# Early loads and an interleaved first projection in an eight-core hybrid decoder step

## The chip, the cores and the metric

The kernel runs on the 8 NeuronCores of one Trainium2 chip. Each core takes one prompt of 2048 positions and 16 single-token samples, 2064 columns in all; no core talks to another. The metric is the device time of the slowest core in microseconds (us). Engines are named as in the profile: PE is TensorE, PEld its weight loads, DVE is VectorE, ACT is ScalarE, POOL is GpSimd, SP the SyncE queue.

Some executions fall in a slow state, in which the cores of one die get a lower clock: 1585.82 us with 0.819 to 0.835 on one die is an example.

## The reference, cut to what matters

Two layers, of which only the first part of the first is touched by the change: RMSNorm, one input projection, a pooling mixer and a short convolution, then the output projection.

```python
def run_group(x, ...):                       # layer 0
    h = rmsnorm(x, norm_mix[0])
    z = h @ w_in_even[0]                     # 1024 -> 512 pool | 512 conv x | 512 B gate | 512 C gate
    p, xb, bg, cg = jnp.split(z, [...], axis=-1)
    a_out, ph = pool_mixer(pool_hist, p, start, w_pool, pool_scale)   # windows 2, 4, 8, 16
    b_out, ch = conv_mixer(conv_hist, xb, bg, cg, conv_w)             # bg * conv3(cg * xb)
    mix = jnp.concatenate([a_out, b_out], axis=-1) @ w_out_even[0]
    x = x + mix
    ...                                      # FFN, layer 1, FFN, final norm: not touched
```

## The kernel before: the parts that matter

x lies feature-major in SBUF, in 8 slabs of 128 features (index `k` or `c`), cut along the columns into five tiles `n` of 256, 512, 512, 512 and 272. A small scheduler gives every instruction the semaphore waits that follow from the buffers that it reads and writes; each engine runs its instructions in the order of the program text. So the order of the text is the order on each engine, and that is what the change moves.

The loads (before):

```python
for q in range(2):                      # x tile 0, two halves, on the SP queue
    x0ev.append(sc.dma("sp", xT[...tile 0, half q], ..., sem=f"xin0_{q}"))
for q in range(2):                      # pooling weights: wait for half 0 of x tile 0
    sc.dma("pool", wring[0][:, q*2048:(q+1)*2048], ..., writes=[wpB[q]], extra=[x0ev[0]])
for q in range(4):                      # x tile 1 in quarters: the first waits for weights half 0
    sc.dma("sp", xT[...tile 1, quarter q], ..., extra=([wpB[0].w] if q == 0 else []))
for n in range(2, 5):                   # x tiles 2 to 4
    sc.dma("sp", xT[:, xrange_(n)], ...)
```

The first projection (before): for all five tiles the pooling products, then four conv chunks `j`, each over five tiles.

```python
spin(18); n_sq(0); n_ones(0); n_apply(0)   # spin: dummy matmuls; n_sq: squares; n_ones: their sum on PE
for n in range(5):                          # n_apply: Ln, Exp on ACT, then 8 products on DVE
    n_sq(n + 1)
    ...                                     # 32 pooling matmuls, n_ones(n + 1) among them (tile 0: after)
    n_apply(n + 1)
    ...                                     # ACT empties the 4 PSUM banks; pooling tasks are set aside
for j in range(4):                          # conv chunks
    if j == 3: use_banks(6)                 # banks 6 and 7 kept for the fold
    for n in range(5):
        ...                                 # x, C, B products: 3 banks, 24 matmuls
        ...                                 # ACT: copy of x; DVE: C * x; ACT: first tap
        for t_ in slots_of.get((j, n), []): tasks.pop(t_)()     # pooling tasks on DVE
        if back: conv_back(*back.pop())     # DVE: two taps, product with B (frees the B bank)
        if j == 3 and n != 2: fold(...)     # 2 matmuls into banks 6 and 7, ACT copies them out
```

Three terms: the dummies (`spin`) are matmuls of ones with zeros that only keep PE at work; a pooling task is DVE's running sum of one channel group over one tile; the fold multiplies `w_pool` and its scale into the output projection's weights, in eight small matmuls.

A matmul result goes to the next of 8 PSUM banks by a counter (`nbank`). A bank can be written again when its last reader is done; this is where PE waits for ACT and DVE.

## Time and profile before

| | before |
|---|---|
| time, median of 4 runs | 1340.77 us (1339.65 to 1341.65) |
| profiled run, slowest and fastest core | 1338.6 and 1334.0 us |
| PE busy in the slowest core | 1298.0 us, 97% |

The prediction below shows the lines and reads them. Two words on how: in a windows table each row is a stretch of time, with the busy time of each engine; in a timeline each row is a group of instructions with its start, its length, and in brackets how long the engine stood idle before it and what released it. For PE a low clock hides in the busy time: 16 matmuls of 512 columns take 3.61 us or, at half clock, nearly twice that, and both count as busy.

### The profile page before, as it was taken

The page shows a single profiled execution, that of the slowest core. Times are in us where ns is not written, and L with a number is a line of the kernel's source. Part 1 is how long each engine was busy: PE and PEld are TensorE (multiplying, and loading weights), DVE is VectorE, ACT ScalarE, POOL GpSimd, SP SyncE. Part 2 cuts the span into 40 slices and gives each one's busy share as a digit, 9 for nine tenths or more (in the row PEclk, how much of TensorE's full clock was granted, in tenths as well). Part 3 has the DMA queues.
Part 4 walks back from the last instruction along what each step waited for, and adds up shares of the span by engine and source line. Part 5 has one row for each costly group of instructions (what it writes and reads, how often), then busy time and mean ns, then how long its engine had stood idle before and what let it go on. Part 6 is the DMA issues. An engine that isn't in the chain of part 4 may idle for free.

```text
span 1338.6 us, 21583 instructions; the slowest of 8 cores (1334.0 to 1338.6 us)
## 1 busy us (share of the span) xinstructions
PE 1298.0 (97%) x7316; PEld 721.1 (54%) x7420; DVE 666.5 (50%) x1167; ACT 346.7 (26%) x668; POOL 169.6 (13%) x220
## 2 busy tenths in 40 slices
PE   6999999999999999999999999999999999999994
PEld 3555545555555555556454665555655556555552
DVE  3588767223527235532764775721262532745266
ACT  2532343111010110012576334411101011010154
POOL 2400153000000000000521005300000000000044
PEclk8999999999999999999999999999999999999998
DMA  8533203122111223102160101221132111220105
GB/s 217 147 62 59 54 1 64 32 44 52 32 32 33 44 53 63 32 16 42 23 127 1 35 5 28 43 53 32 32 58 39 33 32 32 56 40 16 33 33 223
DMA packets 11323, 68.67 MB, mean 51 GB/s; under 512 B 2080, under 2 KB 2208, under 8 KB 5184
## 3 DMA queue, kind: packets, MB, share of 16 engines
q0 software_dynamic: 6912, 47.19, 19.3%
q1 hardware_dynamic: 3728, 19.47, 4.2%
q8 instruction: 63, 1.03, 0.3%
q10 hardware_dynamic: 576, 0.62, 0.1%
q14 instruction: 44, 0.36, 0.1%
HBM read 105.84 MB, written 9.18 MB: 86 GB/s over the span
## 4 chain that ended last, share of the span: by engine, by line
PE 92%; DVE 3%; DMA 2%; issue 2%; ACT 1%; SPq 0%; DVEq 0%; POOL 0%; ACTq 0%; POOLq 0%
PE bank L748 63%; PE bank L818 17%; PE bank L842 5%; PE bank L1173 4%; PE bank L986 2%; DMA xTs<-xT 1%; DVE xTs L671 1%; DMA wring<-wts 1%; PE bank L1229 1%; PE bank L642 0%; DVE xTs L756 0%; PE bank L900 0%; DVE sqall L1070 0%; DVE sqall L1067 0%; DVE gtmp L936 0%
## 5 line engine op out<-in xcount | busy, mean ns | idle before, releaser
L748 PE MATMUL bank<-hTs,wring 128*128 128x512 bf16 (+2 forms) x4105 | 728.8, 337 | 4.0 <-DVE mix L1077 0.9
L748 PEld LDWEIGHTS bank<-hTs,wring 128*128 128x128 bf16 x4160 | 405.4, 98 | 318.5 <-issue 2.8
L799 DVE TENSOR_TENSOR mix<-bank,gtmp 128x512 bf16<-128x512 f32 (+2 forms) x220 | 129.4, 588 | 465.2 <-PE bank L748 459.6
L756 DVE TENSOR_TENSOR xTs<-bank,xTs 128x512 f32<-128x512 f32 (+2 forms) x480 | 278.6, 587 | 89.8 <-PE bank L748 33.8
L796 ACT ACTIVATE gtmp<-bank 128x512 f32<-128x512 f32 (+2 forms) x220 | 112.9, 514 | 712.7 <-PE bank L748 694.6
L818 PE MATMUL bank<-mix,wring 128*128 128x512 bf16 (+2 forms) x1264 | 223.8, 337 | 0.8
L818 PEld LDWEIGHTS bank<-mix,wring 128*128 128x128 bf16 x1280 | 125.3, 98 | 98.0
L125 POOL DMA_DIRECT2D wring<-wts x46 | 25.0, 543 | 941.5 <-PE bank L748 411.6
L631 POOL TENSOR_TENSOR sqall<-sqall 128x512 f32<-128x512 f32 (+5 forms) x110 | 106.5, 968 | 131.6 <-ACT sqall L627 125.2
L748 PE MATMUL bank<-mix,wring 128*128 128x512 bf16 (+2 forms) x632 | 112.9, 337 | 1.7 <-DVE mix L1077 1.2
L748 PEld LDWEIGHTS bank<-mix,wring 128*128 128x128 bf16 x640 | 62.4, 98 | 50.9 <-issue 1.8
L842 PE MATMUL bank<-mix,wring 128*128 128x512 bf16 (+2 forms) x472 | 85.0, 337 | 0.4
L627 ACT ACTIVATE sqall<-xTs 128x512 bf16<-128x512 f32 (+2 forms) x110 | 59.7, 546 | 69.6 <-DVE xTs L756 64.0
L671 DVE SCALAR_TENSOR_TENSOR hTs<-xTs,vecs_s,bank 128x512 bf16<-128x512 f32 (+2 forms) x120 | 73.7, 637 | 1.8 <-ACT bank L652 1.8
L842 PEld LDWEIGHTS bank<-mix,wring 128*128 128x128 bf16 x480 | 47.0, 98 | 36.6
L986 PE MATMUL bank<-hTs,wring 128*128 128x512 bf16 (+2 forms) x158 | 33.0, 369 | 8.1 <-DMA wring<-wts 4.8
L1173 PE MATMUL bank<-mix,hTs 128*128 128x512 bf16 (+1 forms) x135 | 31.9, 379 | 0.1
L1173 PE MATMUL bank<-wring,hTs 128*128 128x512 bf16 (+1 forms) x131 | 31.5, 379 | 0.3
L1217 ACT ACTIVATE gtmp<-bank 128x512 f32<-128x512 f32 (+2 forms) x40 | 20.6, 514 | 42.7 <-PE bank L748 26.6
L748 PE MATMUL bank<-hTs,mix 128*128 128x512 bf16 (+2 forms) x156 | 30.5, 337 | 0.2
L915 DVE SCALAR_TENSOR_TENSOR hTs<-xTs,vecs_s,bank 128x512 bf16<-128x512 f32 (+2 forms) x40 | 22.7, 640 | 15.4 <-ACT bank L911 15.4
L986 PEld LDWEIGHTS bank<-hTs,wring 128*128 128x128 bf16 x160 | 16.6, 106 | 23.6 <-issue 13.0
(95 smaller groups left out, 495.7 us busy)
## 6 DMA issues: line engine op xcount, KB each, us to landing
wring<-wts POOLq DMA_DIRECT2D x38, 1024.0 KB, 8.8
yT<-xTs SPq DMA_DIRECT2D x3, 2048.0 KB, 6.6
xTs<-xT SPq DMA_DIRECT2D x2, 2048.0 KB, 17.9
xTs<-xT SPq DMA_DIRECT2D x6, 512.0 KB, 7.0
wring<-wts POOLq DMA_DIRECT2D x4, 768.0 KB, 7.9
wring<-wts POOLq DMA_DIRECT2D x4, 512.0 KB, 6.4
mix<-wts POOLq DMA_DIRECT2D x2, 1024.0 KB, 18.9
xTs<-xT SPq DMA_DIRECT2D x1, 1088.0 KB, 23.6
```

Source lines behind the costliest of these rows:

```text
L125: E.dma_start(out=out, in_=in_, **kw).then_inc(s, 16)
L627: sc.op("act", lambda E: E.activation(out=rng[i][:, 0:w], in_=xs(c, n), func=AF.Square), reads=[xB[c][n]], writes=[rngB[i]])
L631: sc.op("pool", lambda E: E.tensor_tensor(out=dst[:, 0:w], in0=acc[a][:, 0:w], in1=rng[i][:, 0:w], op=ALU.add), reads=[accB[a], rngB[i]], ...
L671: sc.op("dve", lambda E: E.scalar_tensor_tensor(out=out, in0=xs(c, n), scalar=vecs[:, self.gcol + c:self.gcol + c + 1], in1=r_[:, 0:w], op ...
L748: last = E.matmul(bk[:, 0:w], lhsT=wt[:, o:o + 128], rhs=src_[:, k, c0:c0 + w], start=(k == 0), stop=(k == nk - 1))
L756: sc.op("dve", lambda E: E.tensor_tensor(out=xs(m, n), in0=bk[:, 0:w], in1=xs(m, n), op=ALU.add), reads=[bkB, xB[m][n]], writes=[xB[m][n]])
L796: sc.op("act", lambda E, bg_=bg_, gi=gi, w=w: E.activation(out=gtmp[gi][:, 0:w], in_=bg_[:, 0:w], func=AF.Silu), reads=[bgB], writes=[gtmp ...
L799: sc.op("dve", lambda E, bu_=bu_, gi=gi, w=w, c0=c0, slot=slot: E.tensor_tensor(out=mix[:, slot, c0:c0 + w], in0=bu_[:, 0:w], in1=gtmp[gi] ...
L818: last = E.matmul(bk[:, 0:w], lhsT=wt[:, jl * 1024 + m * 128: jl * 1024 + (m + 1) * 128], rhs=mix[:, slot, c0:c0 + w], start=(jl == 0), st ...
L842: last = E.matmul(bk[:, 0:w], lhsT=wt_[:, jl * 1024 + m * 128: jl * 1024 + (m + 1) * 128], rhs=mix[:, s0 + jl, c0:c0 + w], start=(i == 0), ...
L986: last = E.matmul(bks[g][0][:, 0:w], lhsT=wt[:, k * 512 + g * 128:k * 512 + (g + 1) * 128], rhs=hT[:, k, c0:c0 + w], start=(k == 0), stop= ...
L1173: last = E.matmul(bk[0:ntok, :], lhsT=hT[:, k, t0:t0 + ntok], rhs=wv[:, k * 512:(k + 1) * 512], start=(k == 0), stop=(k == KC - 1))
```

## The change

Its intent is to have PE in steady work earlier and never short of it. The loads of x tile 1, of the pooling weights and of the first conv weights are issued at once on the POOL queue, without waits, in the order in which they are needed. Conv chunk 0 is moved in between the pooling products, so that PE has other work while x tiles 2 to 4 arrive. More dummies bridge the time to tile 1. The last conv chunk keeps all 8 banks, and the fold uses banks that its neighbour tile has freed.

```diff
-        for q in range(2):
-            x0ev.append(sc.dma("sp", xT[:, xrange_(0, 4 * q, 4 * q + 4)], ...))
+        sc.dma("sp", xT[:, xrange_(0)], d_x[:, xrange_(0)], ..., sem="xin0")
...
+        xload(1, 2, "xin1")                     # on the POOL queue, no waits
+        for q in range(4):
+            sc.dma("pool", wring[0][:, q * 1024:(q + 1) * 1024], ...)
+        w_issue()                               # weights of conv chunk 0
+        def late_loads():
+            xload(2, 2, "xin2"); cload("hp", hp, d_hp, eng="pool")
+            xload(3, 1, "xin3"); xload(4, 1, "xin4"); w_issue()
...
+        spin(18); n_sq(0); n_ones(0); n_apply(0, VC_NMIX)
+        spin(34)
+        n_sq(1); late_loads(); ...; n_ones(1); n_apply(1, VC_NMIX)
+        for k in range(4): pool_k(0, k)
+        for n, k in ((0, 4), (0, 5), (1, 0), (1, 1), (0, 6), (1, 2), ...): pool_k(n, k)
+        pool_drain(0); pool_drain(1)
+        n_sq(2, range(4)); conv_front(0, 0); ...; n_sq(2, range(4, 8)); conv_back(...)
+        conv_front(0, 1, late=lambda: n_ones(2)); n_apply(2); early_setup(); rest(); conv_back(...)
+        before = {2: [(1, 0), (2, 0)], 3: [(3, 0), (1, 1)], 4: []}
+        for n in range(2, 5):
+            n_sq(n + 1); pool_banks(n)
+            for k in range(KC): pool_k(n, k)
+            pool_drain(n)
+            for t_ in before[n]: bg.pop(t_)()   # pooling tasks, ahead of n_apply(n + 1) on DVE
+            conv_front(0, n, hook=lambda: n_ones(n + 1))
+            n_apply(n + 1)
+            rest(); conv_back(*bkn)
...
-            if j == 3:
-                use_banks(6)
-                bk, bkB = banks[6 + g % 2], bankB[6 + g % 2]        # in fold
+                bk, bkB = bks[g % 2]                                # the x and C banks of the tile before
```

(Condensed: whole statements are joined on a line, arguments are left out, and the moved buffers of scratch data and the new split of tile 2's squares, part of them now on DVE, are not shown.)

## The prediction

> **What bounds the kernel now.** I read the page first, then the table of windows over the first 150 us, then the waits of the TensorE, then the timeline of the start. The page of before (slowest core):
>
> ```profile
> span 1338.6 us, 21583 instructions; the slowest of 8 cores (1334.0 to 1338.6 us)
> PE 1298.0 (97%) x7316; PEld 721.1 (54%) x7420; DVE 666.5 (50%) x1167; ACT 346.7 (26%) x668; POOL 169.6 (13%) x220
> ...
> PE   6999999999999999999999999999999999999994
> ...
> PEclk8999999999999999999999999999999999999998
> ```
>
> PE is 97% busy; only the first and the last of the 40 slices are below 9. The change touches nothing after the first output projection (about 155 us), so all it can win lies in the first slices. The windows of that stretch (columns: us, then busy us and count of PE, PEld, DVE, ACT, POOL, the granted clock, DMA share, GB/s written):
>
> ```profile
> 0.00:10.00 10.00, 7.68 (x26) 3.12 (x26) 1.52 (x4) 2.93 (x6) 2.81 (x15) 1.00 0.45 114
> 10.00:14.80 4.80, 0.01 (x1) 0.04 (x2) 3.22 (x8) 0.82 (x2) 0.00 (x0) 0.99 1.01 162
> 14.80:24.00 9.20, 9.15 (x50) 5.70 (x51) 0.69 (x1) 1.26 (x2) 1.04 (x1) 0.82 0.97 236
> 24.00:30.50 6.50, 1.85 (x6) 0.49 (x6) 2.37 (x4) 2.96 (x7) 2.11 (x2) 0.84 1.01 328
> 30.50:41.00 10.50, 10.43 (x37) 4.26 (x39) 5.67 (x9) 3.46 (x7) 4.68 (x6) 0.78 0.99 336
> 41.00:63.00 22.00, 21.32 (x115) 11.03 (x115) 13.73 (x27) 11.80 (x25) 10.04 (x12) 1.00 0.50 103
> 63.00:87.00 24.00, 23.84 (x145) 14.09 (x146) 16.72 (x38) 9.61 (x29) 1.97 (x5) 1.00 0.35 65
> 87.00:150.00 63.00, 59.29 (x319) 31.17 (x323) 49.72 (x79) 19.13 (x37) 1.07 (x2) 1.00 0.23 45
> ```
>
> PE's busy time here flatters: 6.80 and 3.40 us of it are the dummy warming matmuls, and at clock 0.78 to 0.84 it does useful work at down to half speed. DMA is half idle in the first 10 us, then saturated to 41 us. The timeline shows why:
>
> ```profile
> 6.98 1.25 POOL L125 DMA_DIRECT2D wring<-wts  x2 [4.84 <-DMA xTs<-xT]
> ...
> 14.79 5.27 PE L986 MATMUL bank<-hTs,wring 128*128 128x256 bf16 x32 [4.83 <-DMA wring<-wts]
> ...
> 26.61 0.63 ACT L885 ACTIVATE sqall<-xTs 128x512 bf16<-128x512 f32 x1 [3.38 <-DMA xTs<-xT]
> ...
> 30.52 5.92 PE L986 MATMUL bank<-hTs,wring 128*128 128x512 bf16 x16 [2.54 <-DVE hTs L915]
> ```
>
> Loads are chained: half of x tile 0, then the pool weights (issued only at 6.98), then x tile 1 (issued when the first weight half lands, 14.6), whose last quarter lands at 26.6 because tiles 2 to 4 queued beside it. PE does 32 matmuls at half clock (14.8 to 20), dummies, scraps, and starts tile 1 at 30.5 cold: 16 matmuls take 5.92 us, where later 16 take 3.61. From 30.5 PE is the bound, less its waits:
>
> ```profile
> PE bank L1048 <- DVE mix L1077: 3.0, 1, 3.0
> PE bank L748 <- DVE mix L1077: 2.1, 3, 1.2
> ```
>
> These (60 to 175 us) are the projection's tail: a fold matmul waits 3.0 us at 129 to 132 for a PSUM bank that a lagging VectorE has not emptied.
>
> **What the Trainium skill says.** *TensorE: Matmul & The Clock Gate*, "What's actually happening": the array runs at half clock until a busy window of about 3.4 us has passed, and falls back after an idle one. The trace agrees in kind: 0.50 at 16 to 18 us after an empty 10.0 to 14.8, 0.50 again at 30.5 after 1.85 busy us in 6.5. *DMA: Bandwidth & Descriptors*, "Queues, rings and completion order": each engine serves the queues in turn and one queue's ring in order. So tile 1 shared with tiles 2 to 4 only by ring order and with weights by turns; arrivals at 20.2, 22.6, 24.2, 26.6 fit. Same page, "Specifications": about 358 GB/s of HBM per core; the saturated windows give 328 and 336. *PSUM — Partial Sum Buffer*, "The four PSUM rules": a start flag clears the accumulation bits of the whole bank, so two 256-wide groups may share a bank if only the first starts it, which is what the changed code does; no run shows more of it yet.
>
> **The change part by part.** (a) Loads. One 1 MB load of x tile 0; at once, on the Pool queue without waits, x tile 1 (2 MB), pool weights (2 MB read, 1 MB written) in quarters, the first conv weights (1.5 MB read); then tiles 2 to 4 behind them. (b) Dummies: 18 as before, then 34 in place of 16. (c) Order: pool products of tiles 0 and 1, then conv chunk 0 of tiles 0 and 1, then for tiles 2 to 4 pool and conv 0 by turns. So PE has conv work while later tiles arrive. (d) One scratch buffer fewer (the conv x is copied straight into the conv buffer and multiplied in place); same count of instructions. (e) Conv chunks keep all 8 banks; the fold uses the two banks that the previous tile freed early. No arithmetic on PE is taken away.
>
> Arrivals, as estimates. x tile 0: before, its bytes flowed from about 2.7 us and it was wholly seen at 8.15. Weights issued at 6.98 began to move at about 9.7, 2.7 later; so tile 1, issued at about 2.1, moves from 4.8. Until then tile 0 has moved 0.5 MB; the other 0.54 MB at half of 330 GB/s takes 3.3 us: done at 8.1, seen at 8.9. Tile 1: 3.15 MB in all, the 2.64 left at 4.8 take 8.0 us: seen near 13.7. Pool weights: 2.1 MB at about 323 read GB/s (162 written in 10 to 14.8, twice that read) 6.5 us: 20; conv 0 weights: 25; tile 2: 31.5.
>
> PE: squares of tile 0 on two engines, 4 x 0.38 = 1.5 us, and its sum of ones ends at 10.7. 34 dummies x 0.216 (3.61/16 less overhead) = 7.3: 18.0. In this time VectorE applies the norm of tile 0 (11.8 to 15.0, 8 x 0.4) and squares its three of tile 1 (3 x 0.69: 17.1), so the ones of tile 1 are free to run: 8 x 0.216 = 1.7: 19.7. Pool tile 0: 32 x 0.109 = 3.5: 23.2. Pool tile 1: 32 x 0.216 = 6.9: 30.1; its inputs come at 0.67 us per k against 0.86 of use. Ones of tile 2: 1.7: 31.9. Before has the same set (pool 0 and 1, ones 0 to 2) done at 41.0. Gain 9.1 us.
>
> From 41.0 to 63.06 before does pool 2 to 4 and ones 3, 4: 6.9 + 6.9 + 3.7 + 1.7 + 0.95 = 20.2 of 22.0 us; the rest are waits for ACT to empty banks. In the new order a cycle takes 4 + 3 + 1 = 8 banks, so pool banks were emptied long ago: gain 1.8.
>
> The fold's 3.0 us wait goes (its banks are emptied by a copy and by the first VectorE product of the tile before), and part of the other 2.1; the first output products still wait for the last conv products, since the last pooling task now stands ahead of them. Gain 3.4.
>
> New stalls: tile 2's normed input comes 0.3 to 0.5 us late after conv 0 of tile 1 (ones in the middle of it, then Ln and Exp 1.3, one apply 0.7, against 1.7 us of PE work left); small bank waits. I allow 1.2. Sum: 9.1 + 1.8 + 3.4 - 1.2 = 13.1 us, 1340.8 - 13.1 = 1327.7; I say 1328.
>
> **The rivals.** *Tile 0 late and PE cold.* If turn-taking brings tile 0 at 11 instead of 8.9, PE is empty from 9.1 to 12.5 and goes cold: 34 dummies then take 7.3 + 2.5 and end near 22.5. The fixed count makes this a loss of 4 us: 1332. For it: tile 0 moved at 240 GB/s before, less than the later rate, and all eight cores start together. Against: tile 1 cannot start before 4.5. *VectorE becomes the bound.* By its rows a conv tile costs it 0.69 + 0.75 + 0.75 + 0.69 = 2.9, a pooling task 1.27 + 0.69; per cycle with a 5.4 apply it has 11.3 of PE's 13.8, and in chunks 1 to 3 about 19.5 of 20.9. That is near; if latencies add, waits of 3 to 5 us return: 1332. Against: before, chunk 0 had the most tasks (20.8) and lost only 0.4. *Transfers bind still.* Tile 2 must be seen by about 34 for its ones at 36.5; my estimate leaves 2.5. At 280 GB/s instead of 330 it comes at 36.5, and PE waits 2 to 3 us, 1330; a Pool queue that can't hold seven loads would be worse. *Better than said:* every wait but 1 us goes and the start holds: 1325.
>
> **Range and chances.** 2% would be 26.8 us. All that PE loses in before is the first 30.5 us less 6.2 of useful work at full clock (ones 0 and 1: 1.0 + 1.7, pool 0: 3.5), 2.3 of cold clock after, and waits of 1.8 and 5.1: 33.5 us; of these at least the 10.7 until tile 0's sums stay, so 2% is out of reach. The rivals cost 2 to 5 us each and more than one may come, so the range is skewed up: 1323 to 1334. Faster by over 2% 0.01, within 2% 0.98, slower 0.01.
>
> **What would show it.** Start: first pool matmul near 19.7 at clock 1.00 (wrong if over 22 or at 0.5); tile 0's first square near 8.9; pool 0 and 1 done near 30. Middle: no wait of pool matmuls for ACT; chunk 1 starts near 74 (before: 84). Tail: no 3 us wait at the fold. After it, the same stages a constant 13 us earlier. I would be wrong if PE waited on x tile 2, if clock under 0.8 stayed past 20 us, or if conv waits on VectorE summed to over 3 us.

## The result, and the profile after

The changed kernel takes 1330.52 us in the median of 10 runs (two of them slow), against 1340.95 of before in the same rounds (15 runs, three of them slow); the fast runs alone have medians of 1330.51 and 1340.79. The ratio of the fast runs is 0.9924, with a 95% interval of 0.9914 to 0.9934: 10.2 us, 0.8% faster. A ratio here is the mean time of one kernel's fast runs over that of the other's in the same rounds, so it is not quite the ratio of the medians. A later measurement of both on one chip gave 1330.32 against 1341.12, 0.9921.

The page of the changed kernel, to be set beside the first fence of the prediction:

```profile
span 1329.0 us, 21718 instructions; the slowest of 8 cores (1327.2 to 1329.0 us)
...
PE   8999999999999999999999999999999999999994
...
PEclk9999999999999999999999999999999999999997
```

The spread of the cores has shrunk too: 1.8 us instead of 4.6. The windows of the same stretches as in the prediction:

```profile
0.00:10.00 10.00, 6.62 (x18) 2.38 (x19) 0.55 (x2) 2.05 (x4) 5.31 (x21) 1.00 0.74 193
10.00:14.80 4.80, 4.80 (x25) 2.43 (x26) 3.19 (x9) 2.74 (x7) 1.04 (x1) 1.00 0.97 280
14.80:24.00 9.20, 9.20 (x56) 5.32 (x55) 4.81 (x10) 1.87 (x3) 5.64 (x7) 1.00 1.08 171
...
30.50:41.00 10.50, 9.81 (x58) 5.41 (x57) 4.36 (x9) 5.86 (x12) 3.08 (x3) 1.00 0.99 337
41.00:63.00 22.00, 20.36 (x94) 9.14 (x95) 19.20 (x33) 7.70 (x16) 8.48 (x9) 1.00 0.34 78
...
```

The clock column is the first thing to see: it is 1.00 in every row, where before it was 0.82, 0.84 and 0.78 from 14.8 to 41 us. The DMA share is 0.74 in the first 10 us instead of 0.45. But from 41 to 63 us PE is busy for 20.36 us of 22, less than before (21.32), while DVE is at 19.20 instead of 13.73: the bottleneck has moved closer to DVE there. The timeline of the start:

```profile
9.44 1.34 ACT L893 ACTIVATE sqall<-xTs 128x256 bf16<-128x256 f32 x4 [5.90 <-DMA xTs<-xT]
...
11.15 7.50 PE L973 MATMUL bank<-mix,ones 128*128 128x512 bf16 x34
...
20.22 10.56 PE L994 MATMUL bank<-hTs,wring 128*128 128x256 bf16 x64
...
56.62 5.56 PE L994 MATMUL bank<-hTs,wring 128*128 128x512 bf16 x25 [1.63 <-DVE hTs L922]
```

L893 is the squaring of x tile 0, L973 the dummies, L994 the pooling products. All 64 pooling matmuls of tiles 0 and 1 run in one piece of 10.56 us from 20.2 us on; before, the first half of them took 5.27 us, part of it at half clock, and the second began at 30.5. The last line is the flaw: pooling tile 3 waits 1.6 us for its first normed slice. The waits of PE up to 175 us in all:

```profile
PE bank L994 <- DVE hTs L922: 2.3, 2, 1.6
...
PE bank L758 <- DVE mix L1068: 1.2, 2, 0.8
PE bank L758 <- DVE mix L961: 0.9, 1, 0.9
PE bank L758 <- ACT wring L1040: 0.9, 1, 0.9
```

The fold's 3.0 us wait of before is gone; a wait for the fold's copies (ACT, L1040), one for the norm (L922) and one for a conv bank (L961, inferred) are new in their places.

To put this in stages, three points are read off the PE timelines of the slowest cores (core 2 before, core 0 after). The third is the start of the run of output-projection matmuls after their last wait for DVE.

| stage ends with | before | after | gain in the stage |
|---|---|---|---|
| pooling of tiles 0 and 1 and the sums of tiles 0 to 2 | 41.0 | 32.5 | 8.5 |
| conv chunk 0 | 83.8 | 77.2 | -1.9 |
| output projection unblocked | 156.24 | 146.53 | 3.1 |
| end | 1338.6 | 1329.0 | -0.1 |

(32.5 is 30.8, where the pooling of tiles 0 and 1 ends, plus 1.7 for the sums of tile 2, which the new order does later. 83.8 is 62.9 plus 120 matmuls at the durations in the prediction, 20.9 us. 77.2 is 76.28 plus eight 272-column matmuls.) From the third point to the end every core of both kernels needs 1181.8 to 1182.8 us, as predicted: the rest is not touched.

### The profile page after: what moved, and what is told of

The parts are those of the page before. It is cut to its first block, busy times and chain, and to the rows that moved or that the text cites. A ratio compares the mean times of both kernels' runs of the same rounds, so it can differ in the third digit from the quotient of the medians.

```text
span 1329.0 us, 21718 instructions; the slowest of 8 cores (1327.2 to 1329.0 us)
## 1 busy us (share of the span) xinstructions
PE 1302.3 (98%) x7438; PEld 721.9 (54%) x7438; DVE 671.4 (51%) x1170; ACT 344.9 (26%) x667; POOL 174.6 (13%) x227
## 4 chain that ended last, share of the span: by engine, by line
PE 92%; DVE 5%; issue 1%; ACT 1%; DMA 1%; DVEq 0%; POOL 0%; ACTq 0%; POOLq 0%
PE bank L758 63%; PE bank L828 17%; PE bank L852 5%; PE bank L1230 4%; DVE hTs L922 1%; DVE xTs L681 1%; PE bank L994 1%; DMA xTs<-xT 1%; PE bank L973 1%; PE bank L1286 1%; PE bank L652 0%; DVE xTs L766 0%; PE bank L907 0%; DVE gtmp L943 0%; DVE sqall L1061 0%
## 5 line engine op out<-in xcount | busy, mean ns | idle before, releaser
L758 PEld LDWEIGHTS bank<-hTs,wring 128*128 128x128 bf16 x4160 | 405.8, 98 | 318.3 <-issue 3.0
L809 DVE TENSOR_TENSOR mix<-bank,gtmp 128x512 bf16<-128x512 f32 (+2 forms) x220 | 129.4, 588 | 465.4 <-PE bank L758 459.8
L125 POOL DMA_DIRECT2D wring<-wts x48 | 25.8, 542 | 915.2 <-PE bank L828 410.3
L681 DVE SCALAR_TENSOR_TENSOR hTs<-xTs,vecs_s,bank 128x512 bf16<-128x512 f32 (+2 forms) x120 | 73.7, 637 | 1.8 <-ACT bank L662 1.7
L994 PE MATMUL bank<-hTs,wring 128*128 128x512 bf16 (+2 forms) x160 | 28.6, 338 | 2.3 <-DVE hTs L922 2.3
L1253 DVE SCALAR_TENSOR_TENSOR R<-mix,rsv 128x1024 bf16<-128x1024 f32 (+1 forms) x17 | 21.8, 1284 | 14.9 <-POOL rsv L1250 14.9
L1306 DVE TENSOR_TENSOR mix<-bank,gtmp 128x512 bf16<-128x512 f32 (+2 forms) x40 | 23.5, 589 | 7.4 <-DVE bank L1297 5.0
```

The source lines that it names most:

```text
L125: E.dma_start(out=out, in_=in_, **kw).then_inc(s, 16)
L681: sc.op("dve", lambda E: E.scalar_tensor_tensor(out=out, in0=xs(c, n), scalar=vecs[:, self.gcol + c:self.gcol + c + 1], in1=r_[:, 0:w], op ...
L758: last = E.matmul(bk[:, 0:w], lhsT=wt[:, o:o + 128], rhs=src_[:, k, c0:c0 + w], start=(k == 0), stop=(k == nk - 1))
L809: sc.op("dve", lambda E, bu_=bu_, gi=gi, w=w, c0=c0, slot=slot: E.tensor_tensor(out=mix[:, slot, c0:c0 + w], in0=bu_[:, 0:w], in1=gtmp[gi] ...
L994: last = E.matmul(bks[g][0], lhsT=wt0[:, k * 512 + g * 128:k * 512 + (g + 1) * 128], rhs=hT[:, k, c0:c0 + w], start=(k == 0 and (w > 256 o ...
```

## The experiments

Eleven kernels, all with correct results, ran in three lots; those of one lot ran on the same chip and share the runs of the kernel before. The medians are of all runs. Where a slow run is among them, the medians of the fast runs are 1340.10 (e3b_foldphase), 1331.41 (e6_nospin), 1336.42 (e3c_foldffn), and 1340.40 and 1341.10 for the kernel before in the first and third lot. The changed kernel itself ran only in the third lot, so smaller differences from it across lots are rough.

| run | what it is | median, us | before, us | ratio, 95% interval |
|---|---|---|---|---|
| e1_loads | changed, order undone | 1339.58 | 1340.43 | 0.9991 (0.9974 to 1.0007) |
| e2_order | changed, loads undone | 1343.80 | 1340.43 | 1.0024 (1.0009 to 1.0039) |
| e3_foldbanks | before, fold part alone | 1340.83 | 1340.43 | 1.0001 (0.9986 to 1.0016) |
| e4_taskslate | changed, tasks later | 1328.68 | 1340.43 | 0.9912 (0.9897 to 0.9927) |
| e3b_foldphase | e3, bank counter set early | 1340.61 | 1341.16 | 0.9994 (0.9978 to 1.0011) |
| e5_sqact | changed, tile 4's squares on ACT | 1329.79 | 1341.16 | 0.9915 (0.9901 to 0.9930) |
| e6_nospin | changed, no second dummies | 1331.94 | 1341.16 | 0.9929 (0.9912 to 0.9945) |
| e7_best | first try at a better version | 1328.64 | 1341.16 | 0.9907 (0.9890 to 0.9923) |
| e3c_foldffn | e3, bank counter set late | 1336.43 | 1341.12 | 0.9967 (0.9954 to 0.9980) |
| e8_best2 | second try | 1326.44 | 1341.12 | 0.9893 (0.9879 to 0.9907) |
| e9_after | changed, unaltered | 1330.32 | 1341.12 | 0.9921 (0.9907 to 0.9935) |

### The loads alone, and the order alone

```diff
 # e1_loads: from the changed kernel
-        conv chunk 0 between the pooling products of tiles 1 to 4
+        pooling products of tiles 2 to 4 first, then conv chunk 0 of tiles 0 to 4
```

> The early loads alone: the changed kernel with the interleaving undone (all pooling products of tiles 0 to 4 first, conv chunk 0 after), its loads, dummies and fold banks kept. If the interleaving is what covers the arrival of x tile 2 (seen near 34 us), PE stands empty from about 30.8 to 38.5 us, goes to half clock once more, and the kernel is 5 to 8 us slower than the changed one: 1335 to 1338. Rival: the interleaving only adds VectorE stalls in the middle (3.3 us in the trace) and the loads are all of the gain: then this is as fast as the changed kernel or faster, 1327 to 1331.

Measured: 1339.58, slower than expected. PE runs out of work when the pooling of tiles 0 and 1 is done:

```profile
19.35 10.56 PE L994 MATMUL bank<-hTs,wring 128*128 128x256 bf16 x63
32.08 0.38 PE L907 MATMUL bank<-sqall,ones 128*128 128x512 bf16 x1 [2.17 <-ACT sqall L893]
...
39.87 4.00 PE L994 MATMUL bank<-hTs,wring 128*128 128x512 bf16 x9 [2.43 <-DVE hTs L922]
...
154.19 13.97 PE L758 MATMUL bank<-mix,wring 128*128 128x256 bf16 x79 [0.80 <-DVE mix L1068]
```

From 29.9 to 39.9 us it does eight sums and nothing else, and the nine matmuls after that take 4.00 us, which is half clock. In the mean of the cores the output projection is unblocked at 153.02, against 145.55 in the changed kernel: 7.5 us later, as expected. The last line shows why the whole is slower than expected: in five of the eight cores, the four slowest among them, the clock falls once more right after the two waits of PE (1.2 and 0.8 us) at the output projection, and the rest takes 1184.0 to 1184.8 us instead of 1182.4 to 1182.8. In the changed kernel such waits (0.9 and 0.8 us) stand there too, but the clock holds, and the stretch of the last line takes 12.31 us. With the order undone nearly the whole gain is lost, although the loads come early. The rival is refuted.

```diff
 # e2_order: from the changed kernel
-        xload(1, 2, "xin1") ... w_issue()          # early, without waits
+        the loads of before, chained; conv weights issued after the squares of tile 1
```

> The order alone: the changed kernel with the chained loads of before (half of x tile 0, then pool weights, then x tile 1 in quarters with tiles 2 to 4 beside it). If the early loads are the 8.5 us of gain at the start, PE begins its steady work near 28 us and the kernel ends at 1338 to 1340, only the tail's 3 us and the missing wait for the banks better, minus the new VectorE stalls. Rival (the start is gained by the dummies and the order, not by the loads): 1330 to 1334.

Measured: 1343.80, slower than the kernel before and than expected. PE begins its steady work at 27.45, and then meets a wait that the order brings with it:

```profile
27.45 11.62 PE L992 MATMUL bank<-hTs,wring 128*128 128x256 bf16 x64
42.67 7.90 PE L756 MATMUL bank<-hTs,wring 128*128 128x256 bf16 x40 [3.61 <-DMA wring<-wts]
```

The interleaved order needs the conv weights at 39 us, some 24 us earlier than the old order did. With the chained loads they are issued at 25.8 and land at 42.5, behind x tile 2 and beside tiles 3 and 4. My placing of their issue is part of this; an issue earlier in the chain would, I think, have taken bandwidth from x tile 1, but no run tries it. As built, the loads without the order give 0.9 us (a difference within its interval), the order without the loads costs 3.4, and together they give 10. Both halves hold the fold part too, which is worth about 3 us (next section), so neither paid by itself. The 3.4 hold only for this placing of the weights.

### The fold's banks, alone

```diff
 # e3_foldbanks: from the kernel before
-            if j == 3:
-                use_banks(6)
-                bk, bkB = banks[6 + g % 2], bankB[6 + g % 2]
+                bk, bkB = bks[g % 2]          # x and C banks of the tile before
```

> The kernel before with one part alone: conv chunks keep all 8 banks and the fold uses the two banks that the previous tile freed. My step says the 3.0 us wait at the fold goes and nothing else: 3 us faster than before, 1337.5 to 1338.5, the PE wait for the fold's bank under 0.5 us. Rival: VectorE is the bound in this stretch and the wait comes back a tile later: 0 to 1 us faster.

Measured: no gain in time. But the trace shows the expected gain and its loss. In the mean of the cores the output projection is unblocked at 151.0 instead of 154.1; from there to the end the cores need 1184.1 to 1186.8 us instead of 1181.8 to 1182.7. The waits of PE after 165 us name the place:

```profile
PE bank L1173 <- DVE ssv L1190: 2.1, 1, 2.1
```

L1173 is the gating layer's projection, 540 us after the output projection. The part alters where the bank counter wraps around, so every later matmul uses another bank than before; by counting the code, the counter stands at 1 instead of 3 at the output projection. At 695 us that makes one matmul meet a bank that is still being read. Three of the cores also fall to half clock for a window after it. Two runs tested whether the counter is the cause.

```diff
 # e3b_foldphase: from e3_foldbanks
+        st_["bank"] = 3
         out_proj("out0", Norm(VC_NFFN + 0, direct=(7,)), out0)
```

> The fold part alone once more, but with the bank counter set to 3 at the first output projection, the value that it has in the kernel before. The first try won 3 us there and lost 2.1 us at a new PE wait near 695 us, in the gating layer. If that wait comes from the position of the bank counter, it is gone now, the time from the unblocked output projection to the end is 1182.3 us again as in the kernel before (1184 to 1187 without this), and the slowest core ends near 1337, 2 to 4 us faster than before. If the wait has another cause, the rest stays at 1184 or more and the time at 1340.

Measured: the wait in the gating layer is gone, but another stands at the start of the output projection (waits of PE after 60 us):

```profile
PE bank L748 <- DVE mix L1078: 4.3, 2, 3.9
```

In this kernel the last conv products sit in other banks than in the kernel before, and a counter set to 3 there leads PE straight to one of them. After that wait all eight cores fall to half clock for a window. So I had set the counter at a wrong place, and the time stayed at 1340.10 (fast runs).

```diff
 # e3c_foldffn: from e3_foldbanks
         merge([wsTB], [SB[3]])
+        st_["bank"] = 1                # the old value, after the output projection
         late_setup()
```

> The fold part alone, with the bank counter set back to its old value only after the first output projection, so that neither the output projection (where the second try met a new wait of 3.9 us) nor the gating layer (where the first met one of 2.1 us) sees another position than it had in the first try or in the kernel before. Expected: the unblocked output projection 3 us earlier in the mean of the cores, as in the first try, 1182.4 us from there to the end on cores without a late half-clock window, and 1.5 to 3.5 us faster than before in all. If it is still within 1 us of before, the 3 us are taken back by something that I have not found.

Measured: 4.7 us between the medians, ratio 0.9967 (2.7 to 6.2 us by its interval), more than expected. All cores need 1181.9 to 1182.5 us after the output projection is unblocked. The size is read more sharply in the stage itself: from the first conv matmul to the unblocked output projection, seven cores of the kernel before need 93.3 us and one 95.0, because its clock falls after the fold's wait; all cores of e3_foldbanks and of e3c_foldffn need 90.4. So the fold part is worth 2.9 us, what its wait says, and the earlier losses came from the position of the bank counter, not from DVE. In the profiled runs the remainder lies before the first conv matmul (59.8 instead of 60.5 us in the mean of the cores), where the two kernels are the same, and in the core that lost clock. In the changed kernel the counter stands at 5 at the output projection (also by counting), and its rest of 1182.4 to 1182.8 shows no such wait.

### The pooling tasks ahead of the norm

```diff
 # e4_taskslate: from the changed kernel
-            for t_ in before[n]:
-                bg.pop(t_)()
             rest, bkn, _ = conv_front(0, n, ...)
             n_apply(n + 1, VC_NMIX)
             rest()
             conv_back(*bkn)
+            for t_ in before[n]:
+                bg.pop(t_)()
```

> The changed kernel with the pooling tasks of chunk 0 moved behind the norm of the next tile and the conv tail in VectorE's order. If the 1.6 us wait for the first normed slice of tile 3 is due to their place ahead of it, that wait goes to under 0.3 us and the kernel gains 1 to 2.5 us: 1328 to 1329.5. Rival: the tasks then sit in front of the next tile's conv products, the same lateness shows up as a wait for the conv bank, and the time stays within 0.5 us of 1330.5.

Measured: 1328.68, 1.8 us faster than the changed kernel (1.6 by its later measurement), as expected. The waits of PE in its core 0, up to 175 us:

```profile
PE bank L758 <- DVE mix L1068: 2.0, 4, 0.8
...
PE bank L994 <- DVE hTs L922: 0.7, 1, 0.7
```

For the normed slices (tile 2) they hold 0.7 us where the changed kernel had 2.3: tile 3's is gone, and so is the 0.9 of L961. The rival is right in part: 0.8 us came back as waits for conv banks (L1068, 2.0 instead of 1.2). Two moved lines were worth a sixth of the whole change.

### Why the tasks were slow: GpSimd beside VectorE

The tasks took far longer in the changed kernel than in the kernel before. DVE in the changed kernel, and in the run that has tile 4's squares on ACT:

```profile
51.38 1.00 DVE L946 SCALAR_TENSOR_TENSOR mix<-R,gtmp 128x256 bf16<-128x256 f32 x1
52.30 0.59 DVE L954 TENSOR_TENSOR small<-gtmp,invc_s 128x3 f32<-128x3 f32 x1
```

```profile
52.26 0.15 DVE L954 TENSOR_TENSOR small<-gtmp,invc_s 128x3 f32<-128x3 f32 x1
52.51 0.17 DVE L957 SCALAR_TENSOR_TENSOR mix<-R,small 128x3 bf16<-128x3 f32 x1
```

Three elements a partition took 0.59 us while POOL squared x beside them:

```profile
52.06 3.25 POOL L897 TENSOR_TENSOR sqall<-xTs 128x272 bf16<-128x272 f32 x4
```

The same four squares take 2.43 us where no such DVE work runs, as in e4_taskslate. The Trainium skill, *SBUF — State Buffer*, section "Who interferes with whom", says that a DVE instruction with two SBUF inputs contends with a GpSimd instruction that reads SBUF, and that one blocks the other for a whole instruction. The run agrees with that:

```diff
 # e5_sqact: from the changed kernel
-                who = (("act", "dve")[c % 2] if n == 0 ...
+                who = "act" if n == 4 else (("act", "dve")[c % 2] if n == 0 ...
```

> The changed kernel with the squares of tile 4 on ACT alone, the order of VectorE untouched. If GpSimd's squares slow VectorE's two-input tasks (1.00, 0.59, 0.49, 0.60 us where before they took 0.43, 0.15, 0.17, 0.16), the tasks are back at the short times, the wait for the first normed slice of tile 3 falls from 1.6 to under 0.4 us, and the kernel gains 1 to 2 us: 1328.5 to 1329.5. If only the place of the tasks matters, the wait stays above 1 us and the time at 1330 to 1330.7.

Measured: the small products are back at 0.15 to 0.17 us and the wait for tile 3's slice is 0.23 us, as expected. The product at L946 still takes 1.00 us, beside POOL's own pooling task, which takes 1.23 us there instead of 1.04. The time is 1329.79, a gain of 0.5 to 0.7 us against the two medians of the changed kernel, less than expected. In the profiles the output projection is unblocked 1.0 us earlier in the mean of the cores (144.55 instead of 145.55): of the 1.4 us won at tile 3's slice, 0.2 went into the PE wait for the conv bank that follows (L961, now 1.1); where the remainder went is not shown. So both were true: the tasks stood in the way, and they were slowed. Taking them out of the way was worth more.

### The dummies

```diff
 # e6_nospin: from the changed kernel
-        spin(34)
+        nbank()
```

> The changed kernel without the 34 dummies (the first 18 stay). Their end sets nothing: the squares of tile 1 end at 18.4 us anyway. If they keep the clock, the first useful products run at a granted clock of 0.5 for one or two windows of 3.4 us and the kernel loses 1.7 to 3.5 us: 1332 to 1334. If they only fill time, it stays within 0.5 us of 1330.5.

Measured: three fast runs from 1330.81 to 1332.47, with a median of 1331.41 (1331.94 with the slow run): 0.9 us slower, between the two expectations. I had overlooked that PE's sums of tile 1 are eight separate matmuls, each of which can begin with its own square. Without the dummies ahead of them they begin earlier but at half clock:

```profile
15.93 3.75 PE L907 MATMUL bank<-sqall,ones 128*128 128x512 bf16 x8 [4.55 <-DVE hTs L922]
19.47 11.63 PE L994 MATMUL bank<-hTs,wring 128*128 128x256 bf16 x64
```

The pooling of tiles 0 and 1 takes 11.63 us instead of 10.56 but starts 0.8 us earlier, and ends at 31.1 instead of 30.8. So the dummies keep the clock and hold up the sums at the same time, and win little.

### Two tries at a better version

```diff
 # e7_best: from e4_taskslate
-        spin(34)                                   +        spin(27)
-  squares of tile 1: ACT 3, DVE 3, POOL 2          +  ACT 5, DVE 2, POOL 1
-  pooling tasks in the slots of the change         +  every later task one slot earlier, none in the last
-  last fold after rest()                           +  last fold before rest()
```

> A version that should beat both: the pooling tasks behind the conv tail (won 1.9 us), every later task one place earlier so that none stands before the last conv products, the last fold's copies ahead of the last conv scaling on ACT, the squares of tile 1 off GpSimd but for one, 27 dummies in place of 34. Expected: first useful products 1.3 us earlier (17.1 instead of 18.5), the waits of 0.9 and 0.8 us at the output projection gone or halved; 1328.7 - 1.3 - 1.2 = 1326.2, between 1325 and 1327.5. If x tile 2 then comes too late, the 1.3 us go back into a wait for its squares: 1327.5.

Measured: 1328.64, no better than e4_taskslate. The pooling products began at 18.2 us, but pooling tile 2 at 40.6, against 41.0 in the changed kernel: between them stand a wait of 0.9 for the pooling weights, and 1.1 for tile 2's norm. So the pooling weights, which land after the products begin, bind as soon as the dummies are cut. The fallback in the expectation was another: a wait for the squares of x tile 2, and the sums of tile 2 wait for nothing (35.86, right after PE's conv work). And the earlier tasks made a new wait of 1.9 us for a conv bank at 98.6 us.

```diff
 # e8_best2: from e4_taskslate
+  spin(29), squares of tile 1 and last fold as in e7_best, slots as in the change
+  the four scaling products for the fold on POOL instead of DVE
+  the last pooling task after tile 0 of the output projection
```

> The version with late tasks, and now: the four scaling products for the fold on GpSimd, the last pooling task behind the first tile of the output projection, the last fold's copies ahead of the conv scaling on ACT, tile 1's squares mostly on ACT, 29 dummies. Expected: waits of 0.4 (chunk 3), 0.9 and 0.8 us (output projection) gone, the start at most 0.4 us earlier because x tile 2 binds: 1328.7 - 1.8 - 0.2 = 1326.7, between 1326 and 1328. If the lateness only moves to the next bank, 1328 to 1329.

Measured: 1326.44, as expected; 3.9 us faster than the changed kernel on the same chip and 14.7 than the kernel before. Its waits of PE up to 175 us are led by tile 2's norm; of those at the output projection 0.2 us for ACT and 0.3 for DVE are left:

```profile
PE bank L997 <- DVE hTs L925: 1.1, 1, 1.1
...
```

> The changed kernel unaltered, as the measure on the same chip: 1330.5 within 0.4 us.

Measured: 1330.32 (1330.13 to 1330.44), as expected; it is the measure for the line above.

## Why the prediction was right, and where its steps were off

The prediction of 1328 within 1323 to 1334 held; 1330.5 was measured. Its sum was 13.1 us of gain; the profiled runs show 9.7 at the output projection. It held because the range had room for one of its rivals to come true, and one did. Step by step:

- **Arrivals.** Tile 0 was estimated at 8.9 us; the cores saw it between 6.84 and 9.44. The four cores that saw it at 9.1 or later are the four slowest of the profiled run, unblocked at 146.2 to 146.5 instead of 144.5 to 145.1. The lateness is carried on, but not by the fixed count of dummies alone: without the second dummies (e6_nospin) the four late cores are still 1.3 us behind the early ones in the mean, against 1.6 with them.
- **Start, 9.1 predicted, 8.5 measured.** The mechanism and the sizes held: first pooling matmul at 20.2 instead of 19.7, clock 1.00 throughout. The 0.6 us are the later arrival and sums.
- **Why it needs both halves.** The prediction spoke of the order as giving PE work while tiles arrive, but did not size it. e1_loads does: without it 7.5 us are lost up to the output projection, and 1.7 more to a clock that falls there.
- **Middle, +1.8 and -1.2 predicted, -1.9 measured.** This is the step that failed: "New stalls: ... I allow 1.2". The stalls from 38 to 77 us were 0.70 + 1.63 + 0.93 = 3.3 us, 2.1 more than allowed; the stage fell short by 2.5, and the other 0.4 is not placed. The first stall was in the working. The other two stalls were the rival *VectorE becomes the bound*, which I had set aside by adding up DVE's busy time (11.3 of 13.8 us in a cycle). The sum was not the question, but what stands ahead of the norm in DVE's order: the pooling tasks, which e4_taskslate moved to win 1.8 us. Besides, I took their durations from a stretch in which POOL was idle; beside POOL's squares they took up to four times as long.
- **Tail, 3.4 predicted, 3.1 measured.** The fold's wait went, and about 2 us remain of waits at the output projection and in chunk 2. The size was right (the fold's part of it alone measured 2.9), though e3_foldbanks shows that it could have been lost on the way: the prediction had no thought of the bank counter's position in later layers.
- **Rest.** Nothing after the output projection changed: 1182.4 us in the slowest core before, 1182.5 after.
- **What the prediction did not see:** the cores of before differ by 4.6 us, and the metric is the slowest. The difference is there when the conv products begin (58.5 to 62.9 us). Two things go with it. The four slowest cores (1, 2, 5 and 7) saw the first half of x tile 0 at 6.45 us or later, the other four at 5.4 or earlier. And each core lost clock for a number of windows: summed over the first 60 us, (1 - clock) times time is 3.4 us in four cores and 5.1 in the other four. The arrival sorts the cores better: core 3 lost 5.1 and is among the fast (1335.1 us), core 1 lost 3.4 and is among the slow (1337.1). After the change the lost clock is 0.0 in all eight, and the cores spread over 1.8 us, although tile 0 arrives over 2.6. The mean of the cores fell by 8.1 us (1336.3 to 1328.2), the slowest by 9.6. The extra 1.5 us come from the smaller spread; whether the loads or the clock made it smaller, no run isolates.

Left open: how much the interleaved order would cost with the chained loads if its conv weights came in time, and how much the early loads would give with the old order if the clock held at the output projection.

## What to carry to other kernels

At the start of a kernel, loads and order belong together: here the early loads were worth next to nothing while PE ran dry before the next tile, and an order that needs other data earlier was worth nothing while that data was not loaded earlier. When an engine's total work fits, still ask what stands ahead of the one result that PE waits for, and take durations from a stretch with the same neighbours. And when a part shows its gain in its own stage and none in the time, look for it hundreds of microseconds later: a rotating buffer counter ties stages together that share nothing else.

## What the Trainium skill lacked or had wrong

- *PSUM — Partial Sum Buffer* has nothing on a rotating bank counter as a link between distant stages. Here a local change moved it and made a wait of 2.1 us 540 us later, and setting it at another place one of 3.9 us; with it set right the same change kept its 2.9 us.
- *TensorE: Matmul & The Clock Gate*, "Seeing it yourself", advises to budget 1.95 GHz (13/16) for dense matmuls on all cores. In fast runs all eight cores hold a granted clock of 1.00 over more than 1200 us of dense bf16 products. The page also says that the limit depends on the data, which no run here varies.
- The same page, in "What's actually happening", says that the cold start varies from run to run and is under 1% of a typical span. Here it is 0.3 to 0.4% (3.4 or 5.1 us lost by (1 - clock) times time). The page has nothing on its differing between the cores of one execution, by 1.7 us here, which counts when the metric is the slowest core.
- *DMA: Bandwidth & Descriptors*, "Specifications", gives about 1 us to the first byte on the POOL queue. Before, weights issued at 6.98 us found the engines idle, and the DMA share was 0.00 from 8 to 9 us and 0.29 from 9 to 10: over 2 us from the start of the issue.
